# Six edits where the two feed-forward layers begin, turn over and end: order, buffers and load times

## The chip, the cores and the metric

The kernel runs on one core of a Trainium2 chip. The measure is the time of one execution on the device in microseconds (us). The kernel before takes 2669.48 us in the median of three runs (2666.13 to 2671.49). The execution whose trace is shown here took 2668.03 us; the trace covers 2666.2 us of it.

The engines have short names in all rows: PE multiplies matrices, DVE is the vector engine, ACT the scalar engine, POOL the general-purpose (GpSimd) engine, and SP issues most of the transfers. Each works through its own list of instructions in order; semaphores hold an instruction until what it needs is there.

## The reference

One layer of a hybrid block is computed for 1024 tokens of width 1024 in float32: a feed-forward layer, a mixer (a recurrence and a banded attention, gated together), a second feed-forward layer, and a small gated projection at the end.

```python
def rms_norm(x, gain):
    return x * rsqrt(mean(x * x, -1) + 1e-6) * gain

def swiglu(h, w_gate, w_up, w_down):            # 1024 -> 2816 -> 1024
    return (silu(h @ w_gate) * (h @ w_up)) @ w_down

x = x + 0.5 * swiglu(rms_norm(x, ffn1_norm), ffn1_w_gate, ffn1_w_up, ffn1_w_down)
h = rms_norm(x, mix_norm)
...                                             # the mixer: merged
x = x + merged @ w_out
x = x + 0.5 * swiglu(rms_norm(x, ffn2_norm), ffn2_w_gate, ffn2_w_up, ffn2_w_down)
x = x + sigmoid(rms_norm(x, ple_norm) @ ple_w_gate) * (p @ ple_w_proj)
```

## The kernel before, in words

**Numbers.** Every float32 operand of a product is split in two parts, `hi` (rounded by ACT, L250) and `lo` (what is left, subtracted by DVE or POOL, L251). One product of two operands is then three matrix instructions: hi·hi, lo·hi and hi·lo (`mm3`, L266 to L268; in the first block of `ffn_up` the same three stand at L427 and L429). Evacuations, sums and splits all run on DVE, ACT and POOL beside PE.

**Feed-forward, up (`ffn_up`).** Gate and up are multiplied by a scheme of seven products M1 to M7 (Strassen's) on 2x2 blocks. The activation side has seven forms F1 to F7, sums of the four quarters B11, B12, B21, B22 of the normalised, transposed input. `forms_0` makes F2 and F4 from the first half of the tokens, and B21; `forms_1` transposes the second half and makes F3, F5, F1, F7, F6 in that order, one `put` before each product. Before the change `forms_1` first gets B11 back by adding the two parts of F2 on POOL (L361, four 128x512 additions). For the first pair of weight blocks (w = 0 is gate, w = 1 is up) the products run as M2, then the transposes of the second half (`next(forms)`), then M4, M3, M5, M1, M7, M6. After that pair a steady loop runs over the other weight blocks.

**From up to down.** `down_first` loads the first 1 MB of activations (`a`, from actD) and of w_down (`b`) in the last turn but one of the loop over matrices; `down_forms0` makes the first two operands of the down product from them (L676 to L681).

**Feed-forward, down (`ffn_down`).** Five groups of eleven steps p: (M5, M3), (M1, M4), M7, M2, M6; a step is one product of 4 x 3 matrix instructions for each M of the group, the operands are made two steps ahead (`forms`, L752). M7's end completes the first half of the tokens, so in group 3 (M2) the first half is normalised (`xnorm`, a short chain of 128x4 DVE instructions, then L320 and L322), and in its steps 3 to 10 it is transposed by `norm_kb`: four transposes on PE (L330), one ACT evacuation (L282) and one DVE evacuation (L283) for each of eight blocks. Group 4 is M6, in which `preload` also splits weights of the next stage.

**Out projection (`out_proj`).** It stands before the second feed-forward layer. When its second column half finishes token block i, `ready(i)` does what the feed-forward needs of it: the sum of squares, `xnorm` of half 0 at i = 3, `forms_0` from i = 5, and at i = 7 `xnorm` of half 1 and the first operands of gate and up (`st_pre_ops`: sum, then the splits of M4's and M2's weights).

**What sets the order.** The program is recorded and then put in order for each engine before it is built; within an engine the order that follows is fixed. Where tiles share a buffer, an instruction waits for the last reader of the tile before it.

Of the kernel before, what the change touches and what calls it, by code (L numbers as in the profile page):

```python
# [18 lines left out]
P = 128  # L19
# [152 lines left out]
class K:  # L172
# [160 lines left out]
    def forms_0(self, F, xn, gcol, nq, pp):  # L333

        V, A = self.nc.vector, self.nc.scalar
        F["B21"] = [self.f32_slot(F, f"f6{2 + q2}", [P, 2, HALF]) for q2 in range(2)]
        for q in range(4):
# [5 lines left out]
            b11 = self.t(nq, [P, HALF], "nta")  # L343
# [87 lines left out]
    def st_pre_ops(self, Rs, nq):  # L431
# [3 lines left out]
        for R, tag in zip(Rs, ("nta", "ntb")):  # L435
            X = self.st_slot()
            t = self.t(nq, [P, HALF], tag)
# [6 lines left out]
    def ffn_up(self, wg, wu, F, R0, ops0, wr, nq, fw, sp, pp, actD, wd, forms):  # L444
# [97 lines left out]
        mul_new([(ss[w], 2, ops0[w]) for w in range(2)])  # L542
# [6 lines left out]
        mul_new([(ss[w], 4, ops0[w]) for w in range(2)])  # L549
# [74 lines left out]
        for i, (p, w) in enumerate(ms):  # L624
# [25 lines left out]
            raw(i + 2)  # L650
            if i == len(ms) - 2:
                last = self.down_first(actD, wd, wr)
# [7 lines left out]
    def down_first(self, actD, wd, wr):  # L660

        b, a = (self.t(wr, [P, 4, HALF], "wr", bufs=2) for _ in range(2))
        self.nc.sync.dma_start(a, actD[0:4, :, 0:HALF].rearrange("c p f -> p c f"))
        self.nc.sync.dma_start(b, wd[0:4 * P, HALF:].rearrange("(c p) n -> p c n", p=P))
        return b, a, {}
# [6 lines left out]
    def down_forms_53(self, hp, s, a, b, fives):  # L672

        V = self.nc.vector
        W = self.st_slot()
# [13 lines left out]
    def ffn_down(self, x, load_x, actD, wd, wr, hp, sp, pp, gcol, first, hT, hook, preload):  # L689
# [126 lines left out]
        for s, (g, p) in enumerate(steps):  # L816
# [16 lines left out]
            if g == 3:  # L833
                if p == 0:
                    xt = [self.t(hp, [P, D], f"h{6 + q}1") for q in range(2)] + [self.t(sp, [P, D], f"x{q}n") for q in "ab"]
                    xn = self.xnorm(x, 0, self.ss, sp, lambda i: xt[i])
# [1101 lines left out]
def kernel(ctx, tc, a, out):  # L1938
# [90 lines left out]
    with ExitStack() as up:  # L2029
# [7 lines left out]
        def ready(i):  # L2037
# [12 lines left out]
            if i == 5:  # L2050
                next(st["f"])
# [62 lines left out]
```

## Time and profile before

| what | value |
|---|---|
| median of three runs | 2669.48 us |
| the execution profiled, and its span | 2668.03 us, 2666.2 us |
| PE busy | 2481.7 us (93%) |
| DVE, ACT, POOL busy | 1613.7 (61%), 977.2 (37%), 1109.9 us (42%) |
| granted clock of PE over the span | 0.9 to 1.0 in tenths of full speed |

PE is busy 93% of the span, and the idle time is not spread evenly. In the loops over matrices it has none; at the places where one stage gives way to the next, the seams, it stands for several microseconds at a time, and after such a stand its granted clock is for some microseconds the lower one of its two levels (1.2 instead of 2.4 GHz). In the slices the clock is written in tenths, and as a mean of a stretch in hundredths.

### The profile page before, as it was taken

The numbers are of one execution on the slowest core, as the hardware profiler recorded it, in microseconds if no ns is written. First come the engines' busy times: TensorE is split into PE (matmuls) and PEld (weight loads), VectorE is DVE, ScalarE is ACT, GpSimd is POOL, SyncE is SP. The second block draws the span as 40 slices with busy tenths as digits, with TensorE's granted clock in tenths as the row PEclk, the third lists the DMA queues.
The fourth block names the chain that finished last, engine by engine and source line by source line (L and its number), as shares of the span: only waits on it lengthen the run. The fifth ranks groups of instructions, "written<-read, shape, count | busy, mean of one in ns | idle before, by whom it ended". The sixth has DMA issues, their size and how long they took to land.

```text
span 2666.2 us, 36580 instructions
## 1 busy us (share of the span) xinstructions
PE 2481.7 (93%) x14285; PEld 2034.9 (76%) x14285; DVE 1613.7 (61%) x2603; ACT 977.2 (37%) x1700; POOL 1109.9 (42%) x625
## 2 busy tenths in 40 slices
PE   6899999999899899999999999789799999989889
PEld 5688888778687677778877988568578888768667
DVE  4865555797823566665448344463765555698852
ACT  5433333333434333333224254223433333333441
POOL 2666565554524233333211011241566565554440
PEclk9899999999999999999999999889899999999999
DMA  5222222655433222222231012751132222453432
GB/s 199 84 90 80 79 96 79 222 175 193 145 128 104 53 76 65 75 69 74 77 132 34 33 49 96 197 200 66 45 103 95 71 88 80 179 212 133 163 109 89
DMA packets 272497, 289.16 MB, mean 108 GB/s; under 512 B 46282, under 2 KB 202540, under 8 KB 272068
## 3 DMA queue, kind: packets, MB, share of 16 engines
q1 hardware_dynamic: 264932, 274.59, 31.5%
q10 hardware_dynamic: 7392, 12.23, 1.4%
q8 instruction: 112, 1.84, 0.3%
q14 instruction: 61, 0.50, 0.1%
HBM read 222.64 MB, written 64.14 MB: 108 GB/s over the span
## 4 chain that ended last, share of the span: by engine, by line
PE 46%; DVE 12%; issue 3%; DMA 3%; POOL 3%; ACT 2%; SPq 0%; DVEq 0%; POOLq 0%; ACTq 0%
PE g L266 7%; PE g L268 6%; PE g L267 6%; PE dn L267 5%; PE dn L268 5%; PE dn L266 5%; POOL wsp L251 2%; PE tr L267 1%; PE tr L266 1%; PE tr L268 1%; DVE X L1126 1%; PE s L1591 1%; DVE sub L1124 1%; PE t L1060 1%; PE po L1634 1%
## 5 line engine op out<-in xcount | busy, mean ns | idle before, releaser
L251 POOL TENSOR_TENSOR wsp<-wr,wsp 128x1024 fp32r<-128x1024 f32 (+1 forms) x158 | 354.0, 2246 | 373.8 <-ACT wsp L250 326.7
L251 POOL TENSOR_TENSOR wsp<-wst,wsp 128x1024 fp32r<-128x1024 f32 x71 | 176.4, 2489 | 477.7 <-ACT wsp L250 401.2
L251 POOL TENSOR_TENSOR wsp<-ws,wsp 128x1024 fp32r<-128x1024 f32 x88 | 220.8, 2511 | 214.9 <-ACT wsp L250 212.5
L266 PE MATMUL g<-h,wsp 128*128 128x512 f32 x496 | 216.4, 436 | 11.8 <-DVE h L1730 7.2
L266 PE MATMUL g<-wsp,h 128*128 128x256 f32 (+1 forms) x664 | 215.0, 324 | 8.0 <-ACT gst L1352 3.5
L267 PE MATMUL g<-wsp,h 128*128 128x256 f32 (+1 forms) x664 | 207.9, 313 | 0.7 <-POOL wsp L251 0.7
L268 PE MATMUL g<-wsp,h 128*128 128x256 f32 (+1 forms) x664 | 207.3, 312 | 0.0
L268 PE MATMUL g<-h,wsp 128*128 128x512 f32 x496 | 200.6, 405 | 2.1 <-POOL wsp L251 2.1
L267 PE MATMUL g<-h,wsp 128*128 128x512 f32 x496 | 200.6, 405 | 0.0
L408 DVE TENSOR_TENSOR ws<-wr 128x512 f32<-128x512 f32 x56 | 86.4, 1552 | 167.0 <-POOL x L251 165.6
L250 ACT ACTIVATE wsp<-ws 128x1024 fp32r<-128x1024 f32 (+1 forms) x110 | 106.4, 967 | 202.9 <-PE tr L268 73.5
L250 ACT ACTIVATE wsp<-wr 128x1024 fp32r<-128x1024 f32 (+1 forms) x158 | 134.3, 852 | 121.6 <-PE g L268 51.9
L266 PE MATMUL dn<-wsp,h 128*128 128x512 f32 x360 | 143.7, 400 | 9.8 <-DVE x L793 5.8
L266 PEld LDWEIGHTS g<-wsp,h 128*128 128x128 f32 x664 | 137.6, 207 | 18.8 <-issue 4.1
L267 PE MATMUL dn<-wsp,h 128*128 128x512 f32 x360 | 142.5, 396 | 6.0 <-POOL wsp L251 6.0
L268 PE MATMUL dn<-wsp,h 128*128 128x512 f32 x360 | 142.0, 396 | 0.1
L267 PEld LDWEIGHTS g<-wsp,h 128*128 128x128 f32 x664 | 138.1, 208 | 4.7 <-POOL wsp L251 0.9
L268 PEld LDWEIGHTS g<-wsp,h 128*128 128x128 f32 x664 | 137.8, 208 | 4.0 <-issue 0.3
L464 DVE TENSOR_TENSOR act<-act,m 128x512 f32<-128x512 f32 x88 | 131.4, 1493 | 1.4
L268 PE MATMUL dn<-h,wsp 128*128 128x512 f32 x320 | 124.8, 390 | 0.0
L267 PE MATMUL tr<-h,wsp 128*128 128x512 f32 x320 | 124.6, 389 | 0.0
L266 PE MATMUL dn<-h,wsp 128*128 128x512 f32 x320 | 124.6, 389 | 0.0
(469 smaller groups left out, 6590.5 us busy)
## 6 DMA issues: line engine op xcount, KB each, us to landing
wr<-ffn_w_down SPq DMA_DIRECT2D x44, 1024.0 KB
wst<-w_in SPq DMA_DIRECT2D x60, 512.0 KB
wr<-ffn_w_gate SPq DMA_DIRECT2D x44, 512.0 KB
wr<-ffn_w_up SPq DMA_DIRECT2D x44, 512.0 KB
actD<-act SPq DMA_DIRECT2D x44, 512.0 KB
a<-actD SPq DMA_DIRECT2D x12, 1024.0 KB
gate<-gst SPq DMA_DIRECT2D x26, 256.0 KB
wst<-ffn_w_down SPq DMA_DIRECT2D x10, 512.0 KB
```

The costliest lines, as they stand in the source:

```text
L250: nc.scalar.activation(dst[:, 0], src, AF.Copy)
L251: (lo_eng or nc.vector).tensor_tensor(out=dst[:, 1], in0=src, in1=dst[:, 0].bitcast(F32), op=ALU.subtract)
L266: mm(ps, lhsT=l[0], rhs=r[0], start=first, stop=False)
L267: mm(ps, lhsT=l[0], rhs=r[1], start=False, stop=False)
L268: mm(ps, lhsT=l[1], rhs=r[0], start=False, stop=last)
L408: self.nc.vector.tensor_tensor(out=out, in0=R[:, i], in1=R[:, j], op=op)
L464: eng.tensor_tensor(out=a, in0=a, in1=v, op=ALU.mult)
L1060: PE.matmul(psd[h][:, i2, e].rearrange("p (a s) -> p a s", a=2), lhsT=BK[hr, i, 2 * e:2 * e + 2].rearrange("p a s -> p (a s)"), rhs=QR[hr, ...
L1124: V.tensor_tensor(out=pr[:, :s + 1, :n], in0=XT[:, :s + 1, s:s + 1].to_broadcast([64, s + 1, n]), in1=at[:, s:s + 1, s + 1:].to_broadcast( ...
L1126: V.tensor_tensor(out=XT[:, :s + 1, s + 1:], in0=XT[:, :s + 1, s + 1:], in1=pr[:, :s + 1, :n], op=ALU.subtract)
L1591: PE.matmul(ps[h][:, pr, :nk * P], lhsT=qT[hr, pr, j * P:(j + 1) * P], rhs=kT[hr, pr, k0:k0 + nk * P], start=True, stop=True)
L1634: PE.matmul(po[pr][64 * h:64 * h + 64, j % 4], lhsT=vt[:, k0 // P + kt, (2 * pr + h) * 64:(2 * pr + h) * 64 + 64], rhs=PT[:, kt, 2 * pr + ...
```

## The change

1. B11 is kept as a tile of its own (tags b110, b111) when `forms_0` evacuates it; the four POOL additions at L361 go.
2. In the first block of `ffn_up` the order is M2 of gate, M4 of gate, M2 of up, then the transposes of the second half, then M4 of up.
3. `st_pre_ops` is called in two halves: gate's operands at i = 4 of the second column half of `out_proj`, up's at i = 7. Their sums go to "wst" buffers, and one weight chunk of `out_proj` goes to a small pool of its own ("wo2"), so that a weight slot is free.
4. `down_first` (the w_down load) moves one matrix ahead of where it was; the activation load stays (`down_second`).
5. In `ffn_down` the eight `norm_kb` move from steps 3 to 10 of group 3 to steps 1 to 8 of group 4.
6. The weight slot of a down step is taken before its sums (no instruction differs by that alone).

```diff
@@ forms_0 @@
+        F["B11"] = [self.f32_slot(F, f"b11{q2}", [P, 2, HALF]) for q2 in range(2)]
...
-            b11 = self.t(nq, [P, HALF], "nta")
+            b11 = F["B11"][q // 2][:, q % 2]
@@ forms_1 @@
-        b12, b11, b22, b21 = [], [], [], F["B21"]
-        for q2 in range(2):
-            b11.append(self.t(sp, [P, 2, HALF], "act", bufs=3))
-            for q in range(2):
-                f = F[2][2 * q2 + q]
-                G.tensor_tensor(out=b11[q2][:, q], in0=f[:, 0].bitcast(F32), in1=f[:, 1].bitcast(F32), op=ALU.add)
+        b12, b22, b21 = [], [], F["B21"]
+        b11 = F["B11"]
@@ ffn_up @@
-        mul_new([(ss[w], 2, ops0[w]) for w in range(2)])
+        for w in range(2):
+            mul_new([(ss[w], 2, ops0[w])])
+            if w == 0:
+                mul_new([(ss[w], 4, ops0[w])])
...
         next(forms)
-        mul_new([(ss[w], 4, ops0[w]) for w in range(2)])
+        mul_new([(ss[1], 4, ops0[1])])
...
+            if i == len(ms) - 3:
+                last = self.down_first(wd, wr)
             if i == len(ms) - 2:
-                last = self.down_first(actD, wd, wr)
+                last = self.down_second(last, actD, wr)
@@ ffn_down @@
-                elif p >= NP - KB:
-                    kb = p - NP + KB
-                    hT[kb][0] = self.half(hp, kb, 0)
-                    self.norm_kb(xn, kb, gcol, hT[kb][0], self.gbank())
+            kb = s - 4 * NP - 1
+            if 0 <= kb < KB:
+                hT[kb][0] = self.half(hp, kb, 0)
+                self.norm_kb(xn, kb, gcol, hT[kb][0], self.gbank())
@@ out_proj and ready @@
-                    W[1].append(self.wcol(w_out, 1, i - 1))
+                    W[1].append(self.wcol(w_out, 1, i - 1, *((po, "wo2", 1) if i == 1 else ())))
...
+            if i == 4:
+                st["ops"] = k.st_pre_ops(st["R"][:1], None)
...
-                st["ops"] = k.st_pre_ops(st["R"], nq)
+                st["ops"] += k.st_pre_ops(st["R"][1:], None)
```

What this does to the order of the engines is shown at three places. The lines of the changed kernel are up to eight higher or lower than those of the kernel before, and the numbers behind the names differ throughout.

First, PE where the second feed-forward layer begins. `dn` are the sums of M4, `g` those of M2, and `tr` receives the transposes of the second half (L330). Before, with M4 of both matrices begun and not yet finished:

```order
L429 MATMUL dn_15905<-h_2387_15654,wsp_15803 128x512
L427 MATMUL dn_15904<-h_2388_15655,wsp_15796 128x512
L429 MATMUL dn_15904<-h_2388_15655,wsp_15796 128x512
L427 MATMUL dn_15905<-h_2388_15655,wsp_15803 128x512
L429 MATMUL dn_15905<-h_2388_15655,wsp_15803 128x512
L330 MATMUL tr_15854<-cst_p_66,f_2408_15788 128x128
L330 MATMUL tr_15859<-cst_p_66,f_2408_15788 128x128
L330 MATMUL tr_15866<-cst_p_66,f_2408_15788 128x128
L330 MATMUL tr_15854<-cst_p_66,f_2409_15790 128x128
L330 MATMUL tr_15859<-cst_p_66,f_2409_15790 128x128
```

The transposes stand behind twelve matrix instructions. In the changed kernel, at the end of gate's M4 and up's M2:

```order
L424 MATMUL dn_15824<-h_2388_15659,wsp_15596 128x512
L426 MATMUL dn_15824<-h_2388_15659,wsp_15596 128x512
L424 MATMUL dn_15824<-h_2385_15656,wsp_15596 128x512
L424 MATMUL dn_15824<-h_2386_15657,wsp_15596 128x512
L424 MATMUL dn_15824<-h_2387_15658,wsp_15596 128x512
L424 MATMUL dn_15824<-h_2388_15659,wsp_15596 128x512
L424 MATMUL g_15837<-h_2382_15648,wsp_15796 128x512
L424 MATMUL g_15837<-h_2383_15649,wsp_15796 128x512
L330 MATMUL tr_15855<-cst_p_66,f_2404_15788 128x128
L330 MATMUL tr_15855<-cst_p_66,f_2405_15790 128x128
L330 MATMUL tr_15855<-cst_p_66,f_2406_15792 128x128
L330 MATMUL tr_15855<-cst_p_66,f_2407_15794 128x128
```

All transposes now follow 36 matrix instructions of M2 and M4, and 32 of them stand nearly together; what was between them before has gone ahead.

Second, DVE in group 3 of the first down product. L322 is the end of `xnorm`, `h<-g` (L283) an evacuation of `norm_kb`, L752 and L251 make the operands of the next steps. Before:

```order
L322 TENSOR_SCALAR h_772_4793<-x_592_3572,nrsy_4798 128x1024
L322 TENSOR_SCALAR xan_4795<-x_594_3574,nrsy_4798 128x1024
L752 TENSOR_TENSOR ws_4912<-a_757_4722,h_699_4179 128x512
L752 TENSOR_TENSOR a_757_4722<-a_609_3600,a_757_4722 128x512
L251 TENSOR_TENSOR wsp_4884<-ws_4885,wsp_4884 128x512
L283 SCALAR_TENSOR_TENSOR h_786_4876<-g_4877,pc_116,h_786_4876 128x512
L752 TENSOR_TENSOR ws_4939<-a_782_4841,h_710_4262 128x512
L752 TENSOR_TENSOR a_757_4722<-a_609_3600,a_757_4722 128x512
L251 TENSOR_TENSOR wsp_4911<-ws_4912,wsp_4911 128x512
L283 SCALAR_TENSOR_TENSOR h_790_4903<-g_4904,pc_116,h_790_4903 128x512
L752 TENSOR_TENSOR ws_4968<-a_782_4841,h_710_4262 128x512
L752 TENSOR_TENSOR a_782_4841<-a_639_3769,a_782_4841 128x512 x2
```

After (L758 is what was L752):

```order
L322 TENSOR_SCALAR h_768_4785<-x_588_3564,nrsy_4790 128x1024
L322 TENSOR_SCALAR xan_4787<-x_590_3566,nrsy_4790 128x1024
L758 TENSOR_TENSOR ws_4888<-a_753_4714,h_695_4171 128x512
L758 TENSOR_TENSOR a_753_4714<-a_605_3592,a_753_4714 128x512
L251 TENSOR_TENSOR wsp_4868<-ws_4869,wsp_4868 128x512
L758 TENSOR_TENSOR a_753_4714<-a_605_3592,a_753_4714 128x512
L758 TENSOR_TENSOR ws_4907<-a_778_4833,h_706_4254 128x512
L251 TENSOR_TENSOR wsp_4887<-ws_4888,wsp_4887 128x512
L758 TENSOR_TENSOR a_778_4833<-a_635_3761,a_778_4833 128x512
L758 TENSOR_TENSOR ws_4928<-a_778_4833,h_706_4254 128x512
L758 TENSOR_TENSOR a_778_4833<-a_635_3761,a_778_4833 128x512
L251 TENSOR_TENSOR wsp_4906<-ws_4907,wsp_4906 128x512
```

The L283 rows have left the stretch; they now stand in group 4, one behind each pair of L758 and L251. On PE the first of the transposes stands 107 rows further on.

Third, ACT in the first block of the first feed-forward layer, where F6 is made (`f<-ws`) and M1's two sums are taken from their banks (L504, which is L501 after). Before:

```order
L250 ACTIVATE f_162_772<-ws_777 128x512
L250 ACTIVATE wsp_813<-ws_814 128x1024
L250 ACTIVATE f_169_821<-ws_819 128x512
L250 ACTIVATE f_170_822<-ws_819 128x512
L504 ACTIVATE ntb_737<-g_711 128x512
L504 ACTIVATE m_152_742<-g_712 128x512
L250 ACTIVATE f_171_823<-ws_829 128x512
L250 ACTIVATE f_172_824<-ws_829 128x512
L250 ACTIVATE wsp_871<-wr_865 128x1024
```

After:

```order
L250 ACTIVATE f_158_764<-ws_769 128x512
L250 ACTIVATE wsp_805<-ws_806 128x1024
L501 ACTIVATE ntb_729<-g_703 128x512
L501 ACTIVATE m_148_734<-g_704 128x512
L250 ACTIVATE f_165_813<-ws_811 128x512
L250 ACTIVATE f_166_814<-ws_811 128x512
L250 ACTIVATE wsp_863<-wr_857 128x1024
L459 ACT_TABLE_LOAD
L459 ACTIVATE act_739<-nta_633 128x512
```

The two evacuations now stand in front of the pair that splits F6, and the second pair of F6 has moved further back.

## Rows read from the trace of the kernel before

**Rows 1.** Busy us (xcount) by stretch: PE, PEld, DVE, ACT, POOL; PEclk, DMA share, GB/s.

```profile
103.00:490.00 387.00, 386.91 (x1698) 319.88 (x1697) 238.92 (x240) 135.28 (x192) 232.13 (x121) 1.00 0.27 89
662.00:707.40 45.40, 37.19 (x164) 29.26 (x165) 43.18 (x57) 25.31 (x43) 24.98 (x15) 0.92 0.52 173
707.40:741.30 33.90, 30.57 (x128) 24.59 (x127) 18.31 (x26) 12.09 (x20) 17.69 (x10) 0.95 0.33 109
1862.00:1890.00 28.00, 20.58 (x96) 15.58 (x95) 18.14 (x26) 15.48 (x28) 13.25 (x11) 0.82 0.11 37
```

**Rows 2.** PE timeline, first down product, groups 3 and 4: start, us, work, [wait <-releaser].

```profile
675.83 0.39 PE L266 MATMUL dn<-wsp 128*128 128x512 f32 x1
681.96 0.69 PE L330 MATMUL g<-cst_p,h 128*128 128x128 f32 x2 [5.74 <-DVE h L322]
...
687.67 0.48 PE L266 MATMUL dn<-wsp 128*128 128x512 f32 x1
...
690.88 0.48 PE L266 MATMUL dn<-wsp 128*128 128x512 f32 x1
...
707.28 0.48 PE L266 MATMUL dn<-wsp 128*128 128x512 f32 x1
...
717.42 0.56 PE L267 MATMUL dn<-wsp 128*128 128x512 f32 x1 [3.33 <-POOL wsp L251]
```

**Rows 3.** Timeline of DVE, group 3 of the first down product.

```profile
684.69 0.75 DVE L283 SCALAR_TENSOR_TENSOR h<-g,pc,h 128x512 fp32r<-128x512 f32 x1 [0.32 <-ACT h L282]
```

**Rows 4.** Timeline of PE, group 3 of the second layer's down product.

```profile
2501.98 0.69 PE L330 MATMUL g<-cst_p,h 128*128 128x128 f32 x2 [5.75 <-DVE h L322]
```

**Rows 5.** Timeline of PE where the second feed-forward layer begins.

```profile
1862.94 0.48 PE L427 MATMUL dn<-h,wsp 128*128 128x512 f32 x1
...
1871.27 1.54 PE L330 MATMUL tr<-cst_p,f 128*128 128x128 f32 x6 [5.34 <-DVE f L322]
...
1888.14 0.51 PE L427 MATMUL tr<-h,wsp 128*128 128x512 f32 x1
```

**Rows 6.** Timelines of DVE, POOL and ACT in the same stretch.

```profile
1865.22 1.20 DVE L238 TENSOR_SCALAR nrsy<-nss 128x4 int32<-128x4 int32 x1
...
1868.89 0.16 DVE L243 SCALAR_TENSOR_TENSOR nrsu<-nrsu,nss 128x4 f32<-128x4 f32 x1
...
1863.42 4.19 POOL L361 TENSOR_TENSOR act<-h 128x512 f32<-128x512 f32 x3
...
1886.85 0.72 ACT L370 ACTIVATE f<-tr,pc 128x512 f32<-128x512 f32 x1
```

**Rows 7.** Timeline of PE where the first feed-forward layer begins.

```profile
55.38 0.50 PE L429 MATMUL g<-h,wsp 128*128 128x512 f32 x1 [1.57 <-POOL wsp L251]
...
78.68 0.51 PE L429 MATMUL dn<-h,wsp 128*128 128x512 f32 x1 [2.36 <-POOL wsp L251]
...
99.36 0.80 PE L427 MATMUL dn<-f,wsp 128*128 128x512 f32 x1 [8.12 <-ACT f L250]
...
102.18 0.63 PE L427 MATMUL g<-f,wsp 128*128 128x512 f32 x1
```

**Rows 8.** Timelines of DVE and ACT in the same stretch.

```profile
63.67 1.23 DVE L381 TENSOR_TENSOR ws<-wst,f 128x1024 f32<-128x1024 f32 x1 [9.91 <-ACT f L370]
...
96.83 0.68 DVE L408 TENSOR_TENSOR ws<-wr 128x512 f32<-128x512 f32 x1
...
97.62 1.06 ACT L250 ACTIVATE wsp<-ws 128x1024 fp32r<-128x1024 f32 x1 [2.60 <-DVE ws L408]
...
100.21 0.59 ACT L504 ACTIVATE m<-g 128x512 f32<-128x512 f32 x1
```

**Rows 9.** Timelines of PE and DVE where up gives way to down.

```profile
497.81 0.50 PE L266 MATMUL g<-wsp,h 128*128 128x512 f32 x1 [1.07 <-DVE m L525]
...
473.24 3.48 DVE L680 TENSOR_TENSOR wr<-wr 128x512 f32<-128x512 f32 x2
490.91 1.64 DVE L680 TENSOR_TENSOR wr<-wr 128x512 f32<-128x512 f32 x2 [5.29 <-DMA wr<-ffn_w_down]
```

More of the change, by code (lines that the diff above doesn't have):

```diff
@@ L436, in st_pre_ops @@
             X = self.st_slot()
-            t = self.t(nq, [P, HALF], tag)
+            t = self.t(nq, [P, HALF], tag) if nq else self.t(self.wp, [P, 1024], "wst", bufs=3)[:, :HALF]
             self.st_sum(t, R, 2)
@@ L656, in ffn_up, with down_first, down_second @@
         return last
-    def down_first(self, actD, wd, wr):
-        b, a = (self.t(wr, [P, 4, HALF], "wr", bufs=2) for _ in range(2))
+    def down_first(self, wd, wr):
+        b = self.t(wr, [P, 4, HALF], "wr", bufs=2)
+        self.nc.sync.dma_start(b, wd[0:4 * P, HALF:].rearrange("(c p) n -> p c n", p=P))
+        return b
+    def down_second(self, b, actD, wr):
+        a = self.t(wr, [P, 4, HALF], "wr", bufs=2)
         self.nc.sync.dma_start(a, actD[0:4, :, 0:HALF].rearrange("c p f -> p c f"))
-        self.nc.sync.dma_start(b, wd[0:4 * P, HALF:].rearrange("(c p) n -> p c n", p=P))
         return b, a, {}
@@ L670, in down_aform, with down_forms_53 @@
         return self.t(hp, [P, 2, HALF], f"h{self.nform % 8}0", dt=F32R)
[L672 removed]
+    def down_forms_53(self, hp, s, a, b, fives, W=None):
         V = self.nc.vector
[L675 removed]
+        W = W or self.st_slot()
         V.tensor_tensor(out=s, in0=a[0], in1=a[1], op=ALU.add)
@@ L754, in forms @@
         def forms(g, p):
+            W = self.st_slot()
             a11, a12, a21, a22 = (aa.get((th, par, p)) for th in range(2) for par in range(2))
@@ L832, in ffn_down @@
             hook(g, p)
[L833 to L836, printed above, removed]
-                elif p >= NP - KB:
-                    kb = p - NP + KB
-                    hT[kb][0] = self.half(hp, kb, 0)
-                    self.norm_kb(xn, kb, gcol, hT[kb][0], self.gbank())
+            if (g, p) == (3, 0):
+                xt = [self.t(hp, [P, D], f"h{6 + q}1") for q in range(2)] + [self.t(sp, [P, D], f"x{q}n") for q in "ab"]
+                xn = self.xnorm(x, 0, self.ss, sp, lambda i: xt[i])
+            kb = s - 4 * NP - 1
+            if 0 <= kb < KB:
+                hT[kb][0] = self.half(hp, kb, 0)
+                self.norm_kb(xn, kb, gcol, hT[kb][0], self.gbank())
             if g == 4:
@@ L1796, in wcol, with out_proj @@
         return self.wchunk(w[q * 256:(q + 1) * 256, n * HALF:(n + 1) * HALF].rearrange("(k p) n -> p k n", p=P), 2, *to)
-    def out_proj(self, mT, x, W, early, sp, pp, ready):
+    def out_proj(self, mT, x, W, early, sp, po, pp, ready):
         nc = self.nc
@@ L2057, in ready @@
                 st["xn"] = k.xnorm(x, 1, st[1], nq, lambda i: k.t(fb, [P, D], f"f7{i}"))
-                st["ops"] = k.st_pre_ops(st["R"], nq)
-        k.out_proj(mT, x, out_["W"], out_["early"], op, pp, ready)
+                st["ops"] += k.st_pre_ops(st["R"][1:], None)
+        with k.pool("po") as po:
+            k.out_proj(mT, x, out_["W"], out_["early"], op, po, pp, ready)
         ops.close()
```

3 lines of the change are left out of this document (1 added, 2 removed).

## The prediction, made blind

> **What bounds the kernel now.** I read the busy time by stretch first. In the loop over matrices PE is busy for 386.91 of 387.00 us, 1698 instructions of 128x512 at 0.228 us each [rows 1]; nothing can be won there except by less work, and the change takes no matrix instruction away. The other stretches are the seams, and there PE is not the bound: 37.19 of 45.40 us in group 3 of the down product, where DVE is busy for 43.18, and 20.58 of 28.00 us at the start of the second feed-forward layer, at a mean clock of 0.82 [rows 1]. Next I read the timeline of PE at each seam for its waits and who ended them, and last the timelines of the engines named there. So the sum is one of waits on PE at four kinds of seam, and of what is late next once a wait is gone.
>
> **Group 3 and 4 of the down product (edit 5, in both layers).** PE's step 4 begins at 675.83; right behind its first instruction stand the first transposes, which wait 5.74 us for the last instruction of xnorm (L322 on DVE). Group 4 begins at 707.28 [rows 2]. So PE takes 31.45 us for steps 4 to 10, which are 7 x 12 instructions, 19.2 us at 0.228. The other 12.3 us are the wait, the eight sets of transposes and a clock that is granted at 0.92 on the mean. One set costs what a step with it takes more than one without: 690.88 - 687.67 = 3.21 against 12 x 0.228 = 2.74, so 0.47, and eight are 3.8 us. They come back in group 4, whose PE is otherwise idle for 3.33 of 33.9 us [rows 1, 2].
>
> With the transposes gone from group 3, DVE is late next. It still has xnorm's short chain between the splits of each step until about 682, and PE's steps come to need a split a step later than now: by the rows of DVE I work out waits of 0.4 to 1.2 us in steps 4 to 8, together 3.5. Eight L283 of 0.75 [rows 3], 6 us, leave DVE's 43.18 there, which is what lets the later steps keep up. Bounds for these waits: 1.5, if DVE catches up after step 5, and 7, if it stays behind at every step (43.18 - 6.0 of DVE against 30.1 of PE in the eleven steps). In group 4 DVE has 18.31 of 33.90 us busy [rows 1], so the L283 are covered there; if that cover fails, each costs up to its 0.75. POOL's weight split (a<-wst) stands one place further back there, behind the split that PE waits for, and of the 3.33 us I give 1.5 back (0 to 3). Sum: 12.3 - 3.5 - 3.8 + 1.5 = 6.5 us (1.5 to 10). The second layer shows the same wait, 5.75 [rows 4], in the same code: again 6.5.
>
> **Start of the second feed-forward layer (edits 1, 2, 3).** From the first M4 instruction at 1862.94 to M3's first at 1888.14, PE takes 25.2 us [rows 5] for 48 instructions (10.9) and 32 transposes (3.8): 14.7 of work. The wait of 5.34 is for xnorm of the second half. Its twelve 128x4 instructions run beside POOL's three L361: three of them take about 1.2 us each, where one alone takes 0.16 [rows 6]. The Trainium skill says why in SBUF — State Buffer, section "Who interferes with whom": DVE and POOL share one pair of ports, and whoever has it holds it for its whole instruction. By that rule the gain of the next sentence falls away if other POOL instructions move into the place of L361, and three splits of gate's and up's operands do stand there in the changed order; they are ready some 3 us before L361 was and end near 1864.9, so that by the rule the sum loses no more than 0.5 us. Without L361 the chain is 3.5 us shorter, and its end comes near 1867.5 instead of 1871.
>
> PE meanwhile does 36 instructions before the transposes, 8.2 us, to 1871.1, because gate's operands are split during the projection and PE need not wait. The 32 transposes then end at about 1875. In the old order the last of them stood behind M2 and M4, and ACT's last evacuation began at 1886.85 [rows 6]. ACT takes up to 0.72 for each of eight, 5.8 us, and can begin about 1872, so it is late next: done at about 1877.8, and with one sum and one split M3 begins near 1879.6 instead of 1888.14. I take 8.5. Upper bound: all slack, 10.5. Lower bound: PE granted the lower of its levels for most of the 36 instructions, 0.456 each and some 6.5 us more: 2. Behind M3 the operands of M5 come from DVE and POOL, whose rows stand in the same order as before; they move with it. Gate's split during the projection puts one more 128x512 split on POOL ahead of the last weight chunk of w_out; POOL is busy for 42% of the whole span, so I cost it at nothing, and at 1.4 us (a third of the row of L361) if that chunk is then late.
>
> **Start of the first feed-forward layer (edits 1, 2).** L361 costs nothing here: DVE idles for 9.91 us until 63.67, waiting for ACT [rows 8]. M2's wait of 1.57 goes, because M4 of gate stands between; but the transposes come 12 instructions later (2.7 us), so that the forms come about 1.2 us later, and the wait of 2.36 at M5 takes up the difference [rows 7]: together nothing, -1.2 to +1.6. The gain is at M7. Its first instruction runs at 102.18 [rows 7], after the evacuations of M1's banks (L504), which end at 100.80; these stand on ACT behind a weight split (97.62, waiting for the DVE sum of 96.83) and behind F6's pair [rows 8]. In the new order two splits less stand on DVE in front of that sum, 0.68 to 1.74 us each by rows of the same shape alone and beside POOL [rows 8, 9], so it comes some 2.3 us earlier, and L504 ahead of F6's pair, two ACT splits, some 1.1: M7 can start near 97.4 and no longer stands behind three M6 instructions, which must still be done later (0.7). 4.8 - 0.7, so 4; 0 to 6 by whether M6's forms, now further back on DVE, stop PE behind M7.
>
> **Up to down (edit 4, both layers).** PE waits 1.07 us for a DVE sum (L525) that is queued behind a w_down subtraction, which waited 5.29 us for its transfer [rows 9]. The first such subtraction, 3.48 us beside POOL [rows 9], goes twelve rows forward into idle time; the evacuations behind it come up to 3.5 us earlier, the activations' h parts free their buffer earlier, and the second w_down load with them. That is about the wait: 1 in each layer, -1 to 3. The load that is now issued last is the activations', 1 MB as w_down's was, and DVE reads it at the same place; if it lands later, DVE stops in front of M5's evacuations, which is the -1. Edit 6 is nothing: no order changes by it.
>
> **Sum.** 6.5 + 6.5 + 8.5 + 4 + 1 + 1 = 27.5 us. The profiled execution took 2668.03 us, so 2640.5 in its terms. It lies 1.45 below the median of the runs, 2669.48; in theirs 2642. All low ends together leave 2 us (2667), all high ends give 43 (2627); either is unlikely.
>
> **Rivals.**
> *The waits are replaced (DVE's limit).* For it: DVE is busy for 95% of group 3, so there the end may be set by DVE's work and not by PE's wait. Then edit 5 saves only the 6.0 us of L283 less 3.8 of transposes, some 2 a layer; edits 1 to 3 save the 3.5 us of the chain; M7's and the seams' gains turn into waits at M6 and at the loads. 2 + 2 + 3.5: 2662. Against it: a good part of those 43 us is DVE instructions that are stretched beside POOL, and after 682 the short chain is over.
> *No change.* M3's forms, M5's weights and M6's forms are late by what came earlier, and each layer's group 4 gives back what group 3 won: 2669.5, give or take 5. For it: the same chain of sums and splits is still there, in the same order. Against it: the rows show PE idle ahead of it, on transposes that are now placed elsewhere.
> *Slower: group 4's transposes stall PE.* PE is in order. If a step's transposes there must wait for their bank until DVE has done the last L283, and this waits behind a split that waits for POOL, each of the sixteen steps can cost what PE's one wait for POOL in that group costs now, 3.33 us: 53 - 27.5 puts it at 2695. It decides from 27.5 / 16 = 1.7 us a step. Against it: DVE, ACT and POOL are idle for about half of group 4 [rows 1].
>
> **How the numbers follow.** The forecast, 2642 with its own range of 2630 to 2656, gets 0.62; DVE's limit, 2656 to 2664, 0.20; no change 0.10; slower 0.08. A change of 0.2%, 5.3 us, is about what a measurement of this kernel can tell from none. So faster 0.82, same 0.10, slower 0.08. The range that leaves out about 2 in 10 is 2627 to 2665.
>
> **What would show it.** Right: no wait over 2 us of PE in group 3, the eight L330 sets inside group 4 at about 3.2 us a step, M3 of the second layer some 16.5 us behind its M4 instead of 25.2, M7 of the first layer starting 4 to 5 us earlier, DVE's 128x4 chain at 0.2 us each. Wrong: waits for DVE in group 3 that add up to over 7 us, waits in group 4 of over 1.7 us a step, M3 waiting for its forms, or PE idle in the loop over matrices, where it was not.

## The result and the profile after

The changed kernel takes 2657.78 us in the median (2654.1 to 2665.55), the kernel before on the same chip 2671.56 (2666.13 to 2681.65): a ratio of 0.9944, 95% interval 0.9925 to 0.9962 (the estimate from the runs; the quotient of the two medians is 0.9948). A second measurement on another chip, beside the last experiments, gave 2653.53 against 2677.6, 0.9914 (0.9887 to 0.994). The forecast was 2642: the direction was right, and the gain was 13.8 us between the medians of the first measurement and 24.1 between those of the second, instead of 27.5.

Where it came from is read off PE's timeline. I cut it at fixed instructions and compare the lengths, in two profiled executions of each kernel. The first layer's start is the last instruction of the embedding, which is here the product `p @ ple_w_proj` (`dn<-wsp,pT`); the second layer's is the last `dn<-wsp,h` of the output projection, six instructions before its end. A loop over matrices ends with its last M3 instruction (`tr<-h,wsp`), and groups 2 to 4 of a down product reach from their first to their last `dn<-wsp`. The gate preload ends with the last `g<-h,a`, the mixer with the last `g<-ya,wsp`.

| stretch of PE, us | before | changed | forecast gain | gain (means) |
|---|---|---|---|---|
| first layer, start and loop | 437.6, 437.6 | 435.9, 436.0 | 4 | 1.65 |
| loop's end to group 2 of down | 141.2, 143.9 | 145.0, 142.6 | 1 | -1.25 |
| groups 2 to 4 | 111.5, 111.9 | 107.1, 107.9 | 6.5 | 4.2 |
| the gate preload behind them | 35.8, 35.9 | 36.3, 36.3 | 0 | -0.45 |
| mixer (no edit) | 997.9, 1005.3 | 1004.0, 1010.6 | 0 | -5.7 |
| second layer, start and loop | 450.5, 450.5 | 440.5, 440.6 | 8.5 | 9.95 |
| loop's end to group 2 of down | 139.2, 142.5 | 139.2, 141.5 | 1 | 0.5 |
| groups 2 to 4 | 112.4, 111.8 | 108.0, 107.4 | 6.5 | 4.4 |
| last stage, up to its first `dn<-wsp,h` | 54.7, 53.4 | 56.5, 56.0 | 0 | -2.2 |

All rows but the mixer together gain 16.8 us (0.63%), inside both intervals. The mixer, which no edit touches, took from 997.6 to 1010.6 us over the fourteen profiles of this study, a scatter nearly as large as the gain. It took 1000.9 us on the mean of the five profiles with the old load order and 1004.1 on the mean of the nine with edit 4; these 3 us are not clear of the scatter, so that the edits leave the mixer alone is not shown.

Busy time by stretch after (us, instructions, clock, DMA share, GB/s), to be held against [rows 1]: loop, group 3, group 4, and the start of the second layer.

```profile
120.00:485.00 365.00, 365.00 (x1612) 302.21 (x1611) 219.57 (x218) 127.00 (x181) 223.63 (x117) 1.00 0.28 89
662.60:705.20 42.60, 34.18 (x134) 25.74 (x133) 38.99 (x50) 21.45 (x36) 28.50 (x15) 0.92 0.58 192
705.20:739.70 34.50, 34.10 (x166) 27.90 (x164) 29.33 (x36) 17.24 (x28) 16.26 (x11) 1.00 0.32 108
1864.10:1892.10 28.00, 23.81 (x120) 18.73 (x118) 19.88 (x31) 19.27 (x32) 13.19 (x9) 1.00 0.11 37
```

Group 3 lost its transposes (134 instructions of PE instead of 164) and yet is only 2.8 us shorter, at the same mean clock of 0.92. Group 4 took the transposes and has almost no idle time left. (The window of group 4 in [rows 1] ends at 741.30, but the group's last instruction starts at 742.95; the whole group takes some 35.9 us there.) At the second layer's start PE's clock is now 1.00 where it was 0.82. This window begins 1.1 us before the projection's last instruction and that of before just behind it; begun at the same place, from 1865.31 to 1893.31, it shows a clock of 0.98 and PE busy for 22.60 us, against 20.58 before.

Timeline of PE, groups 3 and 4 after (start, us, work, [wait <-releaser]), for [rows 2 and 4]:

```profile
678.80 0.50 PE L268 MATMUL dn<-wsp 128*128 128x512 f32 x1 [1.10 <-DVE wsp L251]
...
682.59 0.50 PE L268 MATMUL dn<-wsp 128*128 128x512 f32 x1 [0.61 <-DVE wsp L251]
...
689.86 0.79 PE L267 MATMUL dn<-wsp 128*128 128x512 f32 x1 [4.10 <-POOL wsp L251]
690.45 0.63 PE L268 MATMUL dn<-wsp 128*128 128x512 f32 x1
690.87 0.63 PE L266 MATMUL dn<-wsp 128*128 128x512 f32 x1
691.30 0.63 PE L267 MATMUL dn<-wsp 128*128 128x512 f32 x1
...
712.08 0.50 PE L267 MATMUL dn<-wsp 128*128 128x512 f32 x1 [0.40 <-POOL wsp L251]
...
727.92 0.48 PE L266 MATMUL dn<-wsp 128*128 128x512 f32 x1
...
731.13 0.48 PE L266 MATMUL dn<-wsp 128*128 128x512 f32 x1
...
2501.30 0.80 PE L267 MATMUL dn<-wsp 128*128 128x512 f32 x1 [4.10 <-POOL wsp L251]
```

The waits of 5.74 and 3.33 are gone, and a step of group 4 with its transposes takes 731.13 - 727.92 = 3.21, as forecast. In their place stands a wait of 4.10 for a POOL split, the same in both layers, and behind it instructions follow each other at 0.43 instead of 0.228 us: the lower clock (0.50 granted from 689.90 to 694.20). Over groups 2 to 4 of the first layer PE's waits of over 0.3 us fall from 11.57 to 8.71 us in sum, and the instructions that follow at the lower clock from some fifteen to ten, worth about 1.1 us.

Why POOL is late: timelines of DVE and POOL after, same stretch.

```profile
686.20 0.68 DVE L758 TENSOR_TENSOR ws<-a,h 128x512 f32<-128x512 f32 x1
686.80 0.68 DVE L251 TENSOR_TENSOR wsp<-ws,wsp 128x512 fp32r<-128x512 f32 x1
687.40 0.68 DVE L758 TENSOR_TENSOR a<-a,a 128x512 f32<-128x512 f32 x1
688.00 0.68 DVE L758 TENSOR_TENSOR ws<-a,h 128x512 f32<-128x512 f32 x1
688.72 1.64 DVE L758 TENSOR_TENSOR a<-a,a 128x512 f32<-128x512 f32 x1
...
685.34 6.15 POOL L251 TENSOR_TENSOR wsp<-wr,wsp 128x512 fp32r<-128x512 f32 x2 [5.44 <-PE dn L268]
```

And of POOL and DVE before, at the same place:

```profile
685.30 1.27 POOL L251 TENSOR_TENSOR wsp<-wr,wsp 128x512 fp32r<-128x512 f32 x1 [6.71 <-issue]
...
685.36 1.77 DVE L752 TENSOR_TENSOR ws<-a,h 128x512 f32<-128x512 f32 x1
```

Two splits of POOL that take 1.27 each when they get through take 6.15 together, 4.47 of it the first. DVE meanwhile runs sums and splits with two operands in SBUF, the memory of the tiles, end to end, eight from 683.79, at 0.68 each as if alone. Only at 688.68 does the run break, for less than 0.05 us, and POOL's first split ends 1.1 us behind that break, while DVE's next instruction is the one that is stretched (1.64). Before, the L283 (one operand from PSUM, where PE's sums stand) and waits for ACT stood among them [rows 3]; POOL's split began while an L283 ran and took 1.27, and DVE's next instruction was stretched (1.77). The first split takes 4.46 to 4.47 us in both layers of all seven profiles that have edit 5 or `x1_mid`'s form of it and leave these splits on POOL, and 1.27 to 1.29 in both layers of the four that have the transposes in group 3 as before.

### The profile page after: what moved, and what is told of

It is laid out like the page before. It is cut to its first block, busy times and chain, and to the rows that moved or that the text cites. A ratio compares the mean times of both kernels' runs of the same rounds, so it can differ in the third digit from the quotient of the medians.

```text
span 2657.0 us, 36574 instructions
## 1 busy us (share of the span) xinstructions
PE 2482.9 (93%) x14285; PEld 2035.7 (77%) x14285; DVE 1622.8 (61%) x2603; ACT 976.5 (37%) x1700; POOL 1104.9 (42%) x617
## 4 chain that ended last, share of the span: by engine, by line
PE 46%; DVE 12%; issue 3%; DMA 3%; ACT 2%; POOL 2%; SPq 0%; DVEq 0%; POOLq 0%; ACTq 0%
PE g L266 7%; PE g L268 6%; PE g L267 6%; PE dn L267 5%; PE dn L268 5%; PE dn L266 5%; POOL wsp L251 1%; PE tr L268 1%; PE tr L267 1%; PE tr L266 1%; DVE X L1131 1%; PE s L1596 1%; DVE sub L1129 1%; PE t L1065 1%; PE po L1639 1%
## 5 line engine op out<-in xcount | busy, mean ns | idle before, releaser
L251 POOL TENSOR_TENSOR wsp<-wr,wsp 128x1024 fp32r<-128x1024 f32 (+1 forms) x158 | 356.3, 2260 | 366.1 <-ACT wsp L250 302.7
L251 POOL TENSOR_TENSOR wsp<-wst,wsp 128x1024 fp32r<-128x1024 f32 (+1 forms) x72 | 176.0, 2449 | 507.6 <-ACT wsp L250 421.5
L251 POOL TENSOR_TENSOR wsp<-ws,wsp 128x1024 fp32r<-128x1024 f32 x88 | 219.4, 2494 | 207.8 <-ACT wsp L250 205.4
L266 PE MATMUL dn<-wsp,h 128*128 128x512 f32 x344 | 137.1, 399 | 14.6 <-DVE x L799 9.1
L266 PEld LDWEIGHTS g<-wsp,h 128*128 128x128 f32 x664 | 137.5, 207 | 16.8 <-issue 4.1
L267 PE MATMUL dn<-wsp,h 128*128 128x512 f32 x344 | 136.6, 397 | 6.0 <-POOL wsp L251 6.0
L268 PE MATMUL dn<-wsp,h 128*128 128x512 f32 x344 | 135.9, 397 | 0.1
L266 PEld LDWEIGHTS g<-h,wsp 128*128 128x128 f32 x496 | 97.4, 196 | 36.7 <-DVE h L1735 7.8
```

The source lines that it names most:

```text
L251: (lo_eng or nc.vector).tensor_tensor(out=dst[:, 1], in0=src, in1=dst[:, 0].bitcast(F32), op=ALU.subtract)
L266: mm(ps, lhsT=l[0], rhs=r[0], start=first, stop=False)
L267: mm(ps, lhsT=l[0], rhs=r[1], start=False, stop=False)
L268: mm(ps, lhsT=l[1], rhs=r[0], start=False, stop=last)
```

## The experiments

All ratios are to the kernel before, run on the same chip; stretches are those of the table.

**The norm transposes alone, and all the rest without them.** `e5_only` is the kernel before with edit 5, `no_e5` the changed kernel without it.

```diff
-            if g == 3: ... elif p >= NP - KB: kb = p - NP + KB
+            kb = s - 4 * NP - 1        # e5_only; no_e5 is the reverse, on the changed kernel
```

> The kernel before with the move of the norm transposes alone (edit 5). My prediction gave this edit 13 us (6.5 in each down product), 0.9951 of before. The trace of the changed kernel gives less: groups 3 and 4 together won 4.5 us in the first layer and 3.7 in the second, and the last stage lost 1.8, so about 6 us, ratio 0.9976, with a new PE wait of about 4.1 us on a POOL split (L251) in step 7 of group 3 in both layers. If that new wait belongs to another edit (the earlier w_down load), it is not there and the gain is 13.

> The changed kernel with the norm transposes back in group 3 (all edits but edit 5). By the trace the start of the second feed-forward layer alone won 11 us and the start of the first 3, less what the mixer lost: 8 to 14 us, ratio 0.9948 to 0.9970. It shows also whether the two losses in code that no edit touches come with the other edits: 8 us in the mixer between 985 and 1015 us, and 4.5 us at the end of group 0 in the first layer. If they are drift of single executions, PE reaches the second layer's M2 about 5 us earlier than in the changed kernel's trace; if the edits cause them, it does not. The waits of 5.74 for L322 are back in group 3.

`e5_only`: 2670.53 us, 0.9975 (0.9963 to 0.9988); `no_e5`: 2661.86, 0.9943 (0.9922 to 0.9965). In groups 2 to 4 `e5_only` takes 107.2 and 107.3 us with the waits of 4.10, `no_e5` 111.3 and 111.9 with 5.74 and 3.33 back. So edit 5 alone makes that gain, and the new wait of 4.10 comes with it. It also costs: up to the first `dn<-wsp,h` of the last stage `e5_only` takes 55.9, and `no_e5` 53.4. What `no_e5` was to tell of the mixer stays open: it took 1003.2 us there, near the changed kernel's 1004.0.

**POOL's wait: two remedies.** `x1_mid` lets the transposes begin in step 5 of group 3 (six of the eight sets stand in that group, two in group 4), so that some L283 stand among DVE's splits again; `x2_dve` gives POOL's weight splits of group 3 to DVE.

```diff
-            kb = s - 4 * NP - 1
+            kb = s - 3 * NP - 5                                          # x1_mid
-            self.split(W[:, :, 1], t, lo_eng=G)
+            self.split(W[:, :, 1], t, lo_eng=V if g == 3 else G)         # x2_dve
```

> The changed kernel with the transposes of the norm beginning in step 5 of group 3 instead of step 1 of group 4, when xnorm has ended; three of the eight sets still stand in group 4. My theory: in the changed kernel DVE runs some 5 us of instructions with two SBUF operands without a break, and POOL's split waits for the ports; an L283 (one operand in PSUM) among them gives POOL its turn. The first L283 stands just behind that stretch here, so the wait of 4.1 becomes 2 to 4, and the total is within 3 us of the changed kernel. The rival, that POOL waits because PE released the weight slot late, gives the same 4.1 and the same total.

> The changed kernel with POOL's splits of group 3 (M2 of the down product) put on DVE, so that POOL reads nothing there but two weight splits. If DVE's run of two-operand instructions kept POOL from its ports, PE's wait of 4.1 on POOL goes in both layers, DVE's instructions are no longer stretched (0.68 us each), and the kernel is 4 to 8 us faster than the changed one (0.991 to 0.993 of before), unless DVE with 11 more splits of 0.6 us becomes the bound: then waits of 0.3 us a step for DVE, total as the changed kernel. If POOL was late because its slot came late, DVE is late by the same 4.1.

`x1_mid`: 2655.11, 0.991 (0.9889 to 0.9932), groups 2 to 4 at 108.0 and 109.0: nothing won there. PE's wait is 4.0 us, not the 2 to 4 of my theory but what the rival gives, so that this run does not tell the two apart. Its first L283 (691.47) still comes behind the run of splits, and POOL stands as long:

```profile
684.84 6.16 POOL L251 TENSOR_TENSOR wsp<-wr,wsp 128x512 fp32r<-128x512 f32 x2 [5.45 <-PE g L330]
```

`x2_dve`: 2639.67, 0.9856 (0.9837 to 0.9875), groups 2 to 4 at 100.3 and 99.8, 7 to 8 us less than the changed kernel and more than expected. Windows of its groups 2, 3 and 4:

```profile
628.40:658.50 30.10, 30.10 (x134) 24.58 (x132) 24.97 (x33) 12.13 (x22) 13.32 (x9) 1.00 0.68 227
658.50:692.80 34.30, 31.62 (x133) 24.30 (x132) 31.99 (x61) 21.28 (x36) 6.30 (x2) 1.00 0.70 237
692.80:728.80 36.00, 34.58 (x165) 27.62 (x164) 28.68 (x37) 17.25 (x28) 21.17 (x13) 1.00 0.32 104
```

DVE does 61 instructions in group 3 in 31.99 us where the changed kernel's 50 took 38.99: with POOL down to two instructions it does more work in less time. No wait of PE is over 1 us, and the clock is 1.00. Of the 6.7 us in the first layer 4.8 are waits (8.71 to 3.94), and most of the rest is the clock behind them: two instructions follow at the lower clock where ten did. The rival falls: had the slot been late, DVE would have been late by the same 4.1.

**Does that remedy need edit 5?** `x2_before` is the same line on the kernel before.

> The kernel before with one edit: in group 3 of the down product both parts of the weight are split on DVE, POOL makes none there. The norm's transposes stay in group 3. It tells whether the gain of this edit in the changed kernel (107.1 to 100.3 us and 108.0 to 99.8 for groups 2 to 4) needs the moved transposes. Theory A (the edit takes away the starving of POOL, which before does not have because the L283 stand among the splits; DVE, 43.18 of 45.4 us busy, only gets eleven more splits of 0.68): 111 to 117 us for groups 2 to 4, where before takes 111.5 to 112.4. Theory B (what fills DVE in before is the stretching beside POOL, so that the norm's chain ends earlier without POOL): 104 to 109 us, and the wait of 5.74 for the norm falls to 2 to 4. Ratio 1.000 to 1.004 by A, 0.995 to 0.998 by B.

2672.7, 0.9984 (0.9969 to 0.9998); groups 2 to 4 at 105.7 and 107.6. Theory B holds in the stretch, and its wait falls further than expected; the ratio is a little above its range:

```profile
683.62 0.44 PE L330 MATMUL g<-cst_p,h 128*128 128x128 f32 x2 [1.53 <-DVE h L322]
```

So the kernel before lost to the same contention: there POOL stretched the norm's chain on DVE, here DVE holds up POOL. Edit 5 alone brings 4.3 in the first layer (`e5_only`, 107.2), the remedy alone 5.8, both 11.2; in the second layer 5.1, 4.8 and 12.6. Together they bring somewhat more than their sum.

**Which edit made the second layer's start.** The changed kernel without edit 1, without 2, without 3, and the kernel before with edit 1 alone.

```diff
+            G.tensor_tensor(out=b11[q2][:, q], in0=f[:, 0]..., in1=f[:, 1]..., op=ALU.add)    # no_e1
+        mul_new([(ss[w], 2, ops0[w]) for w in range(2)])    # no_e2: M4 of both behind next(forms)
+                st["ops"] = k.st_pre_ops(st["R"], None)     # no_e3: at i = 7, none at i = 4
+            b11 = F["B11"][q // 2][:, q % 2]                # e1_only, on the kernel before
```

> The changed kernel without edit 1: B11 is made again by the four POOL additions, everything else as changed. From the end of the projection to the last transposes of the loop over matrices the second layer takes 450.4 us in before and 440.5 in the changed kernel. Theory of the prediction (three causes that add): the chain of 128x4 instructions runs beside the POOL additions again and is about 3.5 us longer, so 443 to 445 us here, and in the first layer (435.9 from the last projection of the embedding to the last transposes of the loop) nothing, since DVE idled there. Rival A (edit 1 carries the whole): 448 to 451. Rival B (edits 2 and 3 are enough, the chain is hidden): 440 to 441.5. Time: ratio to before 0.995 to 0.997 by the theory, 0.998 to 1 by A, 0.994 by B.

> The changed kernel without edit 2: M2 of both matrices, then the transposes of the second half, then M4 of both, as before; edits 1, 3, 4, 5 stay. Theory of the prediction: the order decides in the first layer, where the changed kernel won 1.7 us (437.6 to 435.9): here 437 to 438; in the second layer gate's M4 no longer fills the time in which PE waits for the second half's norm, so 2 to 4 of the 9.9 us come back: 442.5 to 444.5 instead of 440.5. Rival A (the order carries the whole): 448 to 451 in the second layer. Rival B (the order is nothing): 440 to 441.5, and 436 in the first layer.

> The changed kernel with the first operands of gate made again where those of up are made (behind the last token block of the projection); edits 1, 2, 4, 5 stay. Theory of the prediction: gate's first product then waits for its splits, which stand among the second half's norm on DVE; 2 to 4 of the 9.9 us come back, 442.5 to 444.5 in the second layer; the first layer is as in the changed kernel (435.9). Rival A (edit 3 carries the whole): 448 to 451. Rival B (it is nothing): 440 to 441.5.

> The kernel before with edit 1 alone (B11 kept, no POOL additions). From the end of the projection to the last transposes of the loop the second layer takes 450.5 us in before, 446.5 in the changed kernel without edit 1, 440.5 in the changed kernel and 440.1 and 439.0 without edits 2 and 3. Theory (edit 1 is enough there; edits 2 and 3 each find nothing left to win): 439 to 442 here. Rival (edit 1 needs one of the others): 443 to 447. In the first layer before takes 437.6, the changed kernel without edit 2 440.0: theory (edit 1 without the new order costs there): 439 to 441; rival: 436 to 438. Ratio to before 0.996 to 0.998 by the theory.

| kernel | us | ratio | first layer | second layer |
|---|---|---|---|---|
| no_e1 | 2658.36 | 0.9928 (0.9905 to 0.9951) | 437.3 | 446.5 |
| no_e2 | 2660.11 | 0.9944 (0.9926 to 0.9963) | 440.0 | 440.1 |
| no_e3 | 2654.12 | 0.9929 (0.9907 to 0.9951) | 436.0 | 439.0 |
| e1_only | 2664.36 | 0.9945 (0.9928 to 0.9962) | 438.4 | 440.1 |
| before, changed | | | 437.6, 435.9 | 450.5, 440.5 |

In the second layer edit 1 alone gives the whole 10 us; without it the other edits still give 4. They do not add: what edits 2 and 3 win without edit 1 is part of what edit 1 wins alone. So the theory for `no_e1` was too small (446.5, not 443 to 445), Rival B holds there for `no_e2` and, with 439.0 below its range, for `no_e3`, and the theory for `e1_only` holds there. In the first layer it is the other way round: edit 1 without edit 2 costs (0.8 in `e1_only`, 2.4 in `no_e2`, against before), edit 2 without edit 1 gives 0.3 (`no_e1`), and together they give 1.7. I had expected nothing of edit 1 there, 437 to 438 for `no_e2` and 439 to 441 for `e1_only`, and missed all three. The trace of `e1_only` has the cost in one wait, of PE for M6's operands, which was 8.12 before [rows 7] (and is 12.41 in `no_e2`):

```profile
97.79 0.80 PE L424 MATMUL dn<-f,wsp 128*128 128x512 f32 x1 [11.36 <-ACT f L250]
```

Why that wait grows without the new order is not settled. The ratios of `no_e1` and `e1_only` lie below their expected ranges. The whole times of these kernels do not tell them apart, since their intervals overlap; only the stretches do.

How `no_e1` loses 6 us, POOL, DVE and then PE at the second layer's start:

```profile
1862.84 4.23 POOL L361 TENSOR_TENSOR act<-h 128x512 f32<-128x512 f32 x3
...
1864.64 1.21 DVE L238 TENSOR_SCALAR nrsy<-nss 128x4 int32<-128x4 int32 x1
1865.89 1.21 DVE L240 TENSOR_SCALAR nrsy<-nrsy 128x4 int32<-128x4 int32 x1
1867.13 1.19 DVE L242 TENSOR_TENSOR nrsu<-nrsy 128x4 f32<-128x4 f32 x1
...
1871.34 0.80 PE L427 MATMUL g<-h,wsp 128*128 128x512 f32 x1 [3.74 <-DVE h L347]
```

The same in the changed kernel:

```profile
1868.54 0.17 DVE L238 TENSOR_SCALAR nrsy<-nss 128x4 int32<-128x4 int32 x1
...
1870.52 0.16 DVE L244 SCALAR_TENSOR_TENSOR nrsy<-nrsu,nrsy 128x4 f32<-128x4 f32 x1
...
1872.13 0.50 PE L424 MATMUL g<-h,wsp 128*128 128x512 f32 x1 [0.63 <-DVE h L348]
...
1882.15 0.39 PE L424 MATMUL tr<-h,wsp 128*128 128x512 f32 x1
```

Beside the additions on POOL, and the split behind them, three instructions of DVE's chain are 1.04 us longer each, 3.1 together, and PE waits 3.1 us longer (3.74 - 0.63). Most of the rest comes behind the wait: the next twelve matrix instructions, from 1871.34 to 1876.62, start 0.44 us apart instead of 0.228 (granted clock 0.50), another 2.5.

**What repeats.** Both kernels once more.

> The kernel before, a second execution with a profile, on another day's chip than its first. Between the profiles of before and after, stages that no edit touches differ: from the last weight-matrix instruction of the gate preload (g<-h,a) to the last g<-ya the mixer takes 997.9 us in before and 1004.0 in after; from the first instruction of the down product to that of its group 2 the first layer takes 133.4 in before and 137.5 in after; from the loop's end to the down product it takes 7.9. Theory (these are differences from one execution to the next): here the mixer takes 1001 to 1005 us, and groups 2 to 4 of the down product, which are edited, take 111 to 112.5 in both layers as in the first profile. Rival (the edits moved the mixer, through the weight buffers that it takes over): the mixer takes 997 to 999 again.

> The changed kernel once more, beside the others on one chip. Theory (differences in stages that no edit touches are from one execution to the next): the down product up to its group 2 in the first layer, 137.6 us in its first profile and 133.3 in before, may come out anywhere between 131 and 138; the mixer's four parts (124.4, 464.3, 70.6 and 344.7) together within 998 to 1006; the edited places repeat to 0.5 us: 435.9 and 440.5 for the two starts, 107 and 108 for groups 2 to 4. Rival (the edits set them): 137.6 again. Ratio to before 0.9935 to 0.9955.

`before_again`: 2680.42 us, mixer 1005.3, groups 2 to 4 at 111.9 and 111.8. `after_again`: 2653.53, 0.9914 (0.9887 to 0.994), mixer 1010.6 (above what I had allowed), the stretch up to group 2 142.6 instead of 145.0. The edited starts and groups repeat within 0.9 us (0.5 was expected); the mixer does not, in either kernel. What it depends on is open. The first profile of before also had a lucky place, between the loop and the down product, [rows 9]; PE and DVE in `before_again`:

```profile
501.28 0.79 PE L266 MATMUL g<-wsp,h 128*128 128x512 f32 x1 [4.08 <-DVE m L525]
...
491.32 3.94 DVE L680 TENSOR_TENSOR wr<-wr 128x512 f32<-128x512 f32 x2 [5.24 <-DMA wr<-ffn_w_down]
```

Here the wait is 4.08 instead of 1.07. From the loop's end to the first instruction of the down product it is about 11 us in seven of the ten layers run with the old load order, and 6.6 to 7.5 in sixteen of eighteen with edit 4. On the means that is 9.87 against 8.02 us in the first layer and 10.35 against 7.27 in the second. Of these 1.9 and 3.1 us, 1.0 and 2.6 are left at the start of group 2 (144.3 to 143.3, 142.4 to 139.8). Single profiles scatter there over 4 to 7 us, so the first layer's 1.0 is not clear of chance. Edit 4 was not run alone; it is the one edit besides edit 6, which changes no order, that all of the eighteen have and none of the ten.

**A version that beats both.** `best` is `x2_dve` with edit 3 undone and a buffer of its own for the third sigmoid of the last stage.

```diff
-                sg = self.t(sp, [P, HALF], "ws", bufs=2)
+                sg = self.t(hp, [P, D], "h71")[:, :HALF] if (n, i) == (0, 2) else self.t(sp, [P, HALF], "ws", bufs=2)
```

> The changed kernel with three more edits that the runs so far point to: in group 3 of the down product both parts of the weight are split on DVE (as in the run before that had this alone, whose groups 2 to 4 took 100.3 and 99.8 us instead of 107.1 and 108.0); the first operands of gate and up are made together again (edit 3 undone, 439.0 instead of 440.5 in the second layer's start); and the third sigmoid of the last stage goes to a buffer of its own, so that it no longer waits 6.0 us for the store of the first. Theory: the three add: groups 2 to 4 at 100 in both layers, 439 for the second layer's start, and from the end of the down product to the last stage's next part 53 instead of 57.0 us, with PE's wait for L283 there under 1.5 us instead of 4.46. Ratio to before 0.981 to 0.986. Rival: DVE's order around the first tail L283 is what costs, not the buffer: the wait stays at 4 us, 57 us, and the ratio at 0.985 to 0.988.

2639.31, 0.9849 (0.9834 to 0.9863), groups 2 to 4 at 100.0 and 99.9, the last stage at 53.4 instead of the 57.0 of `x2_dve`. Undoing edit 3 gained nothing here (440.6). The buffer's 3.6 us stand in the trace, but by their times `best` and `x2_dve` can't be told apart; the 439.0 of `no_e3` did not come again, so edit 3 is worth nothing that shows in either direction. What held the last stage in the changed kernel (ACT, DVE, PE):

```profile
2575.01 0.60 ACT L1885 ACTIVATE ws<-dn 128x512 f32<-128x512 f32 x1 [6.07 <-DMA out<-ws]
...
2575.64 0.69 DVE L1886 TENSOR_TENSOR ws<-ws,xan 128x512 f32<-128x512 f32 x1 [2.17 <-ACT ws L1885]
2576.24 0.74 DVE L283 SCALAR_TENSOR_TENSOR h<-g,pc,h 128x512 fp32r<-128x512 f32 x1
...
2577.04 1.11 PE L330 MATMUL g<-cst_p,a 128*128 128x128 f32 x4 [4.44 <-DVE h L283]
```

and in `best` (ACT, PE):

```profile
2554.26 0.60 ACT L1885 ACTIVATE h<-dn 128x512 f32<-128x512 f32 x1 [1.55 <-PE dn L268]
...
2558.57 0.66 PE L330 MATMUL g<-cst_p,a 128*128 128x128 f32 x4 [2.23 <-DVE h L283]
```

The sigmoid no longer waits for a store, and PE's wait halves, to 2.23 us; under 1.5 was expected.

## Why the prediction was right in direction and too large

The forecast summed 27.5 us; the stretches of the table gained 16.8. By its own terms:

- **Groups 3 and 4, 6.5 each; measured 4.2 and 4.4.** The step that failed is "by the rows of DVE I work out waits of 0.4 to 1.2 us in steps 4 to 8, together 3.5". DVE's waits were inside their bounds and half of that: 1.10 and 0.61. What was missing is POOL, whose split in group 3 I had put at nothing: I had taken out the L283 as load on DVE and not seen that they, and the waits around them, were where POOL came through. That put in 4.10 us and the lower clock behind it, so that the sign "no wait over 2 us of PE in group 3" did not come. The 3.33 in group 4 went almost wholly (0.40 left), 1.4 more than I had taken. The bounds, 1.5 to 10, held.
- **Second layer's start, 8.5; measured 9.95.** The mechanism holds: the 128x4 chain at 0.16 to 0.17 each, its last row at 1870.52 although the projection ends 3.3 us later than in the first profile of before, M3 16.9 us behind the projection's last instruction instead of 26.2. That I shared it among three edits was wrong: edit 1 alone does it, so that 8.5 came near is in part luck. What POOL's splits cost the chain in the place of L361 was weighed rightly, at no more than 0.5 us: one instruction lost 0.43 (L314, 0.60 instead of 0.17). In group 3 I had not asked the same question. The Trainium skill, SBUF — State Buffer, "Who interferes with whom", says that a DVE instruction with two SBUF inputs contends with a POOL instruction that reads SBUF, and that the order of issue decides who waits. The trace agrees with the first half: in group 3 POOL stood beside such instructions, 6.15 us for two splits. The second half does not tell how long: POOL's split began at 685.34, and the five DVE instructions that began behind it, from 685.59 to 688.00, still ran ahead of it, at 0.68 us each.
- **First layer's start, 4; measured 1.65.** M7 begins 43.7 us behind the embedding's last instruction instead of 49.5, 5.8 earlier and more than the 4.8 taken. Then the case of the lower bound came about: M6's forms lie further back on DVE. PE, then DVE, after, for [rows 7 and 8]:

```profile
95.44 0.79 PE L424 MATMUL g<-f,wsp 128*128 128x512 f32 x1 [6.20 <-ACT ntb L501]
...
112.62 0.50 PE L424 MATMUL dn<-f,wsp 128*128 128x512 f32 x1 [1.88 <-ACT f L250]
...
98.78 0.68 DVE L503 TENSOR_TENSOR nsq<-ntb,m 128x512 f32<-128x512 f32 x1
...
110.69 1.21 DVE L378 TENSOR_TENSOR ws<-b,wst 128x1024 f32<-128x1024 f32 x1
```

  Before, the last sum of these forms stood ahead of DVE's row of sums for M1 and M7; now it stands behind it (110.69), and the second M6 waits. In the sum I had put that wait at nothing: the 0.7 there is for three M6 instructions that must be done later, and only the lower bound allowed for the wait. Of the 5.8 us 1.65 are left, so 4.2 were lost: beside the 0.7 the wait of 1.88 and some 1.6 for the lower clock behind it (0.58 granted from 113.90 to 118.00).
- **Up to down, 1 each; measured -1.25 and 0.5** on these pairs, 1.0 and 2.6 on the mean of all profiles. The wait that edit 4 attacks is larger than my one profile showed (1.07 there, 4.08 in another execution). Its gain on the means is above the 1 that I took in the second layer, and in the first not clear of the scatter. The bounds, -1 to 3, held on the means.
- **What was not in the sum:** the last stage, -2.2, and the preload, -0.45. Edit 5 alone causes both (`e5_only` and `no_e5` above; the preload takes 36.3 in the one and 35.8 in the other): DVE's first L283 of the last stage stands behind a multiplication that waits for the sigmoid, and that for a store, where before it stood ahead of that multiplication (2584.38 against 2586.60). I had followed the edit to the end of group 4 and not to the stage behind it.

The rival "DVE's limit" (2656 to 2664) named a time that the first measurement's 2657.78 meets, while my own range, 2630 to 2656, ends just below it. But the rival met it neither by its cause nor by its sum: group 3 was held by POOL standing beside DVE, the savings at the second layer's start came in full, and the stretches gained 16.8 us where its sum has 7.5. The slower rival is refuted by group 4's 34.10 busy of 34.50 us.

## What to carry to other kernels

When work is taken off a busy engine, ask what its pauses were good for: here a run of DVE instructions with two SBUF operands and without a gap held up POOL for over 4 us, and giving POOL's share to DVE then shortened both. Price a wait of PE with the lower clock behind it. Take the edited stretches from two executions of the kernel before, and follow an edit one stage further than its code.

## What the runs showed of the hardware that was not expected

- Two POOL splits of 128x512 took 6.15 us beside a run of two-operand DVE instructions, against 1.27 for one that came through. DVE's own instructions kept 0.68 us up to 688.68, and only the two behind that lost about 1 us each (1.64 and 1.76). A break of less than 0.05 us in DVE's run was enough for POOL; beside an L283 it needed none.
- With POOL down to two instructions in group 3 DVE did 61 instructions in 31.99 us, with fifteen on POOL 50 in 38.99.
- A PE wait that was 3.1 us longer cost 6 in all (`no_e1`): 2.5 of the rest are twelve instructions at the lower clock behind it.
- An unedited stretch of 1000 us varied by 13 us between the profiled executions, in kernels with and without the edits.
